# Expert weights in 2 MB tiles, down projections behind the group loop

## The chip, the cores and the metric

The kernel runs on one core of a Trainium2 chip. The metric is device time in microseconds (us) of one execution. A profiled execution also gives a trace of every instruction and transfer; its times are given in us from the start of the span, the span being the time from the first to the last instruction.

## The reference, cut to what matters

Two layers of a transformer-like trunk over 256 tokens of width 1024, all in float32. Each layer has a mixer part (attention with latent keys and values, a stick-breaking attention, a pooling mixer, fed by one input projection and closed by one output projection) and a part of experts: 4 groups of 8, of which each token uses two, so that nearly all experts have some tokens and all their weights are read.

```python
def hybrid_layer(x, ...):
    hn = rms_norm(x, norm1_g)
    proj = jnp.einsum('bsd,df->bsf', hn, w_in)            # 1024 x 1440
    ya = mla_mixer(...); yb = stick_breaking_mixer(...); yc = pool_mixer(...)
    x = x + jnp.einsum('bsm,md->bsd', jnp.concatenate([ya, yb, yc], axis=-1), w_out)
    return x + hier_moe(rms_norm(x, norm2_g), w_group, b_group, w_expert, b_expert, w_gate, w_up, w_down)

def hier_moe(h, ...):                                     # combine: weight of each expert for each token
    ...
    for g in range(N_GROUPS):
        a = jnp.einsum('nd,edf->nef', t, w_gate[g])       # 8 experts, 1024 x 256 each
        b = jnp.einsum('nd,edf->nef', t, w_up[g])
        hid = jax.nn.silu(a) * b * combine[:, g, :, None]
        y = y + jnp.einsum('nef,efd->nd', hid, w_down[g]) # 256 x 1024 each
```

The experts' weights are 96 MB a layer, the other weights of a layer some 12 MB (10^6 bytes); everything is read from HBM once.

## The kernel before

**Weights.** All weights pass through a ring (`Ring`) of 25 slots of 1 MB in SBUF (128 partitions x 2048 float32), which also holds the intermediate tiles (`take`). The order of the transfers, the stream, is written out in `Net.__init__`: w_in (`wa`, `wqk`, `wvu`), the small weights, `uq`, w_out (`wo`), then for each of 8 groups of 4 experts 8 tiles of gate and up weights and 4 tiles of down weights. For the last four groups (`TAIL`) of a layer the down tiles come behind all gate and up tiles, sorted by column quarter, and between the quarters stand the next layer's `wa` and `wqk`. SP issues the transfers. A first, empty pass of the program (`rehearsed`) finds for each transfer the earliest step at which a slot is free for it until its use; in the real pass `tick` issues it there, and SP waits on the chip until the slot's last reader is done.

**Mixers.** The input projection splits weights and activations into two parts each, so that three fast matmuls make one exact one: `split` turns a piece of a weight into its two parts (ScalarE and VectorE, or VectorE and GpSimd), up to three pieces ahead (`AHEAD`). `project_in(l, q, part)` multiplies rows 2q and 2q+1 of `wa` (part 0, 1) and `wqk` (part 2, 3) as soon as column quarter q of x is there. `mixers` then does the eight row blocks of the values and of the pooled part (`values_in`), between the steps Abs, Exp and Ln of the stick-breaking on ScalarE, then head keys, values and queries, attention and the output projection. `route` ends it: routing, and the tokens of the first group gathered into 4 x 32 places (`gather`, by a matmul with a placing matrix d from `place`).

**Experts.** `experts` goes over the 8 groups. `hidden(g)` multiplies 8 tiles; four experts share the array, 32 columns each. `bend` applies SiLU and the expert weight, `collect(g + 1)` gathers the next group's tokens from `hv`, a normalised copy of x, `turn` transposes. For groups 0 to 3 `whole` does the down projection (4 tiles) and adds it to x with a plain matmul (`dT`). Behind group 3 stands `overflow`, a branch for experts with over 32 tokens, not taken here; it claims 5 slots. Groups 4 to 7 keep their hidden values (`th`, `tail`); behind the loop their down projections run by column quarter: `down(g, q)` of one tile, its split into two parts, a scatter of four fast matmuls to the tokens, and once a quarter of x is done, `arrive(l + 1, q)` transposes it for the next layer, whose `project_in` parts run between the items of the next quarter. In the last layer the finished quarter goes to the final norm instead (`leave`), and two idle matmuls stand behind each item (`warm`). The last tile of the stream comes in two halves.

## Time and profile before

| | us |
|---|---|
| median of 3 runs | 603.17 |
| runs | 601.71 to 604.39 |
| the profiled execution | 601.43 |
| its span | 599.8 |
| busy in the span: PE | 526.3 |
| VectorE (DVE) | 261.2 |
| ScalarE (ACT) | 142.7 |
| GpSimd (POOL) | 96.6 |

The transfers are 228.68 MB, of which 93.3% of the 16 transfer engines' time in the span is taken by the queue that SP fills. A matmul's end is modelled in the records, so a busy PE isn't one at its peak, and rows that follow each other may overlap a little. PEclk is the share of the full clock that TensorE was granted: 1.00 is 2.4 GHz, 0.50 is 1.2 GHz.

### The profile page before, as it was taken

What the parts mean: (1) busy time and instruction counts of PE and PEld (TensorE: products, weight loads), DVE (VectorE), ACT (ScalarE), POOL (GpSimd) and SP (SyncE); (2) the same over time, 40 slices, a digit from 0 to 9 for tenths busy, and PEclk for the clock granted to TensorE, in tenths of its full rate; (3) what the DMA queues carried; (4) which work ended last, traced back from release to release, by engine and by line L of the source; (5) the groups of instructions that cost most, each with busy time, mean ns of one, the idle gap of its engine ahead of it and who ended that gap; (6) DMA issues with size and microseconds to landing.
All of it is one profiled execution on the core that took longest, in us unless ns stands there. A gap on an engine that the chain in (4) does not pass through costs nothing. (4 is left out here: it accounts for less than half of the span.)

```text
span 599.8 us, 10395 instructions
## 1 busy us (share of the span) xinstructions
PE 526.3 (88%) x4168; PEld 332.7 (55%) x4168; DVE 261.2 (44%) x644; ACT 142.7 (24%) x339; POOL 96.6 (16%) x138
## 2 busy tenths in 40 slices
PE   8989999898898688679999899998898868886993
PEld 8959877454354144326667787765344424441562
DVE  5879765432332222215357976662332321221242
ACT  4466453200000000013234854322000000001221
POOL 2535223000000000002113442310000000000011
PEclk9999999989999799959999999998999998997998
DMA  8999777999999999999999958689999999999992
GB/s 300 402 419 413 294 281 306 368 389 423 420 420 422 414 422 422 418 423 417 422 419 421 412 200 325 273 325 392 415 423 421 419 419 421 419 422 423 420 398 89
DMA packets 34619, 228.68 MB, mean 381 GB/s; under 512 B 3841, under 2 KB 6145, under 8 KB 7938
## 3 DMA queue, kind: packets, MB, share of 16 engines
q1 hardware_dynamic: 34130, 227.33, 93.3%
q8 instruction: 36, 0.59, 0.4%
q10 hardware_dynamic: 432, 0.59, 0.3%
q14 instruction: 21, 0.17, 0.1%
HBM read 226.85 MB, written 1.05 MB: 380 GB/s over the span
## 5 line engine op out<-in xcount | busy, mean ns | idle before, releaser
L224 PE MATMUL ps<-slot,slot 128*32 128x256 f32 (+6 forms) x3372 | 406.9, 438 | 53.9 <-DVE slot L780 23.2
L224 PEld LDWEIGHTS ps<-slot,slot 128*32 128x32 f32 (+2 forms) x3372 | 242.8, 143 | 187.2 <-issue 94.6
L242 POOL TENSOR_TENSOR slot<-slot,slot 128x512 fp32r<-128x512 f32 (+1 forms) x38 | 50.9, 1339 | 131.0 <-DVE slot L290 54.6
L288 ACT ACTIVATE slot<-ps 128x256 fp32r<-128x256 f32 (+5 forms) x70 | 33.2, 474 | 142.3 <-PE ps L224 128.4
L833 DVE TENSOR_REDUCE ws<-ps 128x1 f32<-128x256 f32 x16 | 6.8, 425 | 131.1 <-PE ps L282 131.1
L224 PE MATMUL ps<-slot 128*128 128x256 f32 (+3 forms) x224 | 58.8, 406 | 0.0
L830 ACT ACTIVATE slot<-ps 128x256 f32<-128x256 f32 x16 | 6.1, 384 | 209.5 <-PE ps L224 209.5
L809 POOL TENSOR_TENSOR slot<-slot,comb 128x128 f32<-128x128 f32 x32 | 12.2, 401 | 266.0 <-PE ps L224 224.8
L242 DVE TENSOR_TENSOR slot<-slot,slot 128x512 fp32r<-128x512 f32 (+1 forms) x54 | 47.4, 880 | 13.9 <-ACT slot L288 13.5
L224 PEld LDWEIGHTS ps<-slot 128*128 128x128 f32 (+1 forms) x224 | 30.2, 193 | 30.8 <-issue 14.4
L793 DVE TENSOR_TENSOR slot<-ps,vec 128x512 f32<-128x512 f32 x32 | 22.1, 692 | 49.5 <-PE ps L224 49.2
L290 DVE COPY slot<-ps 128x512 f32<-128x512 f32 (+3 forms) x30 | 20.5, 690 | 40.9 <-PE ps L224 32.6
L242 DVE TENSOR_TENSOR slot<-ps,slot 128x256 fp32r<-128x256 f32 (+1 forms) x42 | 18.3, 435 | 43.3 <-ACT slot L288 43.2
L288 ACT ACTIVATE slot<-slot 128x512 fp32r<-128x512 f32 (+1 forms) x54 | 33.0, 613 | 15.8 <-PE ps L224 12.8
L282 PE MATMUL ps<-ident,slot 128*128 128x128 f32 x128 | 24.3, 295 | 5.0 <-DVE slot L835 2.9
L282 PEld LDWEIGHTS ps<-ident,slot 128*128 128x128 f32 x128 | 14.8, 144 | 24.2 <-issue 15.4
L863 DVE TENSOR_TENSOR x<-x,ps 128x512 f32<-128x512 f32 x32 | 22.0, 688 | 8.5 <-PE ps L224 8.2
L224 PE MATMUL ps<-ident,ones 128*128 128x128 f32 x108 | 19.1, 312 | 1.6 <-POOL ident L193 1.6
L244 DVE SCALAR_TENSOR_TENSOR slot<-ps,vec,slot 128x256 fp32r<-128x256 f32 x26 | 12.4, 482 | 17.9 <-ACT slot L288 17.8
L288 ACT ACTIVATE slot<-ps,vec 128x256 fp32r<-128x256 f32 x26 | 12.1, 474 | 27.6 <-PE ps L282 13.2
L290 DVE CAST slot<-slot 128x512 fp32r<-128x512 f32 (+1 forms) x38 | 18.5, 487 | 0.0
L224 PEld LDWEIGHTS ps<-ident,ones 128*128 128x128 f32 x108 | 16.0, 216 | 4.0 <-issue 2.4
(126 smaller groups left out, 303.5 us busy)
## 6 DMA issues: line engine op xcount, KB each, us to landing
slot<-in_we SPq DMA_DIRECT2D x191, 1024.0 KB, 19.6
slot<-in_wo SPq DMA_DIRECT2D x8, 1024.0 KB, 19.2
slot<-in_wvu SPq DMA_DIRECT2D x4, 1024.0 KB, 19.8
slot<-in_wqk SPq DMA_DIRECT2D x3, 1024.0 KB, 19.3
slot<-in_wa SPq DMA_DIRECT2D x3, 832.0 KB, 14.2
slot<-in_uq SPq DMA_DIRECT2D x2, 1024.0 KB, 15.2
slot<-in_small SPq DMA_DIRECT2D x2, 784.0 KB, 15.5
x<-in_x SPq DMA_DIRECT2D x4, 256.0 KB, 6.3
```

The source lines that it names most:

```text
L224: self.nc.tensor.matmul(out, lhsT, rhs, start=start, stop=stop, skip_group_check=True)
L242: V.tensor_tensor(lo, in_, hi.bitcast(F32), op=OP.subtract)
L244: V.scalar_tensor_tensor(lo, in_, scale, hi.bitcast(F32), op0=OP.mult, op1=OP.subtract)
L282: self.nc.tensor.transpose(out, in_, self.ident)
L288: nc.scalar.activation(out, in_, AF.Copy, scale=1.0 if scale is None else scale)
L290: nc.vector.tensor_copy(out, in_)
L793: self.nc.vector.tensor_tensor(xs[:, 4 * n:4 * n + 4], v3(self.ps[:, b0 + n], 4, 128), self.vec[:, l, 8 + 4 * n:12 + 4 * n, None].to_broad ...
L809: G.tensor_tensor(d4, d4, comb[:, t, 4 * g:4 * g + 4, None].to_broadcast([128, 4, 32]), op=OP.mult)
L830: A.activation(h, ps[:, 2, 0:256], AF.Silu)
L833: V.tensor_reduce(ws, ps[:, 3, 256:512], axis=AX.X, op=OP.add)
L863: V.tensor_tensor(xs, xs, ps[:, 6 + n], op=OP.add)
```

## The change

- The ring has 11 slots of 2 MB ("pairs") and 3 of 1 MB ("ones"); all weights come in tiles of up to 2 MB (4096 floats a partition), and intermediate tiles that belong together (xH and xL, wH and wL, kT and qT, sH and sL, mH and mL) share a pair. The first tile of the stream comes in three parts, the last in three.
- Groups 0 to 3 have no `whole` any more: the down projections of all 8 groups run behind the loop by column quarters, 32 items a layer.
- Between the items of quarters 1 to 3 of the first layer stands more of the next layer's projection: besides `project_in`'s parts (the two of `wqk` cut in halves) two row blocks of `values_in` a quarter (`behind`). So of layer 1's eight blocks six are done ahead of `mixers`, which then fills the stick-breaking's gaps with head keys, values and queries. There `down` writes one bank (2) instead of two in turn, and the scatter follows in the same item.
- `collect` gathers from x with a scaled placing matrix (`place` makes two: plain and times r2); `hv` is gone, and `overflow` moves from group 3 to behind group 7 and claims three pairs.

```diff
-NSLOT = 25
+NPAIR, NONE = 11, 3
 AHEAD = 3
-TAIL = 4
...
+        r.cut = {"a0.0": ((0, 928),), f"d33.{L - 1}": ((0, 2048), (2048, 3072), (3072, 4096))}
+        rest = [lambda c=c: r.part(*r.stream[0][0:2], *c) for c in ((928, 1856), (1856, 3712))]
+        w(0, "a0", then=[rest[0], load_x(1), rest[1], load_x(2), load_x(3)])
+        w(0, "a1", then=[self.tables])
+        w(0, "v")
         for l in range(L):
-            w(l, "wvu", 0, 1)
-            add(f"sm.{l}", a["small"][l])
-            add(f"uq.{l}", a["uq"][l])
-            w(l, "wo", 3, 2, 0, 1)
-            for g in range(8 - TAIL):
-                we(l, g, *range(12))
-            for g in range(8 - TAIL, 8):
-                we(l, g, *range(8))
+            w(l, "mid", "w0", "w1")
+            for g in range(8):
+                for i in range(4):
+                    add(f"h{g}{i}.{l}", a["wh"][(l * 8 + g) * 4 + i])
             for q in range(4):
...
+                for p in range(4):
+                    add(f"d{q}{p}.{l}", a["wd"][(l * 4 + q) * 4 + p])
+                if l + 1 < L:
+                    w(l + 1, *(("a0", "v"), (), ("a1",), ())[q])
+                elif q == 1:
+                    add("fg", a["fg"])
...
+    def behind(self, q):
+
+        for i in range(2):
+            self.project_in(q, i)
+            yield
+        for i in range(2):
+            w = self.weight()
+            for b in range(2):
+                self.heads_in(2 * q + i, w, (2 * b, 2 * b + 1))
+                yield
+        for i in range(2):
+            self.values_in(2 * q + i)
+            yield
...
+        blocks = deque(range(6 if l else 0, 8))
+        self.values_in(blocks.popleft())
...
+        if l:
+
+            ring.drop("xHL")
+            sH, sL = (v3(t, 4, 384) for t in ring.two("sHL", F32R))
+            values_out()
+            fill = deque([lambda: keys(0), lambda: keys(1), latent_values,
+                          *(lambda j=j: latent_queries(j) for j in range(4))])
+        else:
+            fill = deque([*(lambda k=k: self.values_in(k) for k in blocks)])
...
+    def place(self, g, d, t, pos, r2):
+
+        V = self.nc.vector
+        V.tensor_tensor(d[:, t].rearrange("p (e s) -> p e s", e=4),
+                        self.iota[:, None, :].to_broadcast([128, 4, 32]),
+                        pos[:, t, 4 * g:4 * g + 4, None].to_broadcast([128, 4, 32]), op=OP.is_equal)
+        V.tensor_scalar(d[:, 2 + t], d[:, t], r2[:, t:t + 1], None, op0=OP.mult)
...
-            if i < 0:
-                whole(g, hT, dT)
-            else:
-                tail[g] = hT, dT
-                ring.drop(f"g{g}")
+            turn(g, hT[:, g])
+            ring.drop(f"g{g}")
...
-            if g == 3:
-                self.overflow(l, hv, comb, pos, flag)
-        ring.drop("hn")
+        self.overflow(l, r2, comb, pos, flag)
...
+            beside = self.behind(q - 1) if more and q else None
+            for g in range(8):
+                b = ps[:, 2 if beside else (2, 7)[g % 2], 0:256]
+                down(g, q, b)
+                ys = [parts[:, g % 2 * 2 + p] for p in range(2)]
                 self.parts(*ys, b)
+                if beside:
+                    next(beside)
+                    scatter(g, ys)
+                    continue
                 if prev:
                     scatter(*prev)
-                if l + 1 == L and (q, g) != (3, 7):
+                if not more and (q, g) != (3, 7):
                     self.warm(2, 3)
                 prev = (g, ys)
-                if q and l + 1 < L:
-                    self.project_in(l + 1, q - 1, i)
```

## Rows read from the trace of the kernel before

**Rows 1.** The page: span, transfers, throughput in 40 slices of 15 us (GB/s).

```profile
span 599.8 us, 10395 instructions
...
GB/s 300 402 419 413 294 281 306 368 389 423 420 420 422 414 422 422 418 423 417 422 419 421 412 200 325 273 325 392 415 423 421 419 419 421 419 422 423 420 398 89
DMA packets 34619, 228.68 MB, mean 381 GB/s; under 512 B 3841, under 2 KB 6145, under 8 KB 7938
```

**Rows 2.** Stage table: window and its us; busy us of engines (instructions); PEclk, DMA share, GB/s.

```profile
0.00:58.00 58.00, 53.26 (x331) 47.57 (x331) 43.76 (x85) 32.21 (x67) 25.04 (x38) 1.00 0.98 385
58.00:130.00 72.00, 68.87 (x516) 51.15 (x514) 39.11 (x133) 26.30 (x71) 16.95 (x26) 0.98 0.84 322
130.00:240.00 110.00, 94.12 (x797) 43.63 (x793) 30.80 (x62) 3.71 (x8) 3.80 (x10) 0.97 1.01 420
240.00:340.00 100.00, 86.65 (x679) 57.51 (x678) 49.03 (x108) 33.58 (x77) 20.56 (x20) 0.93 1.01 421
340.00:425.00 85.00, 81.87 (x597) 60.50 (x599) 50.66 (x149) 30.37 (x78) 21.17 (x28) 0.98 0.81 314
425.00:580.00 155.00, 131.51 (x1164) 65.54 (x1156) 40.62 (x90) 12.10 (x28) 6.50 (x14) 0.94 1.01 421
580.00:588.00 8.00, 8.00 (x96) 5.54 (x96) 3.65 (x9) 2.05 (x6) 0.90 (x1) 1.00 0.66 245
```

**Rows 3.** Waits of SP's queue, 345:360: us in total, times, longest.

```profile
SPq L80 <- PE ps L224: 17.6, 1, 17.6
```

**Rows 4.** Timeline of PE (start, us, what): first experts; last output projection, layer 1.

```profile
110.45 7.07 PE L224 MATMUL ps<-slot,slot 128*32 128x512 f32 x64
...
388.97 0.96 PE L224 MATMUL ps<-slot,slot 128*128 128x512 f32 x3
...
400.57 7.07 PE L224 MATMUL ps<-slot,slot 128*32 128x512 f32 x64
```

**Rows 5.** Timeline of PE, layer 0: last hidden tile, then items of quarter 0.

```profile
257.27 1.93 PE L224 MATMUL ps<-slot,slot 128*32 128x512 f32 x8 [1.41 <-DMA slot<-in_we]
...
264.28 1.93 PE L224 MATMUL ps<-slot,slot 128*32 128x256 f32 x16 [0.46 <-DMA slot<-in_we]
...
267.30 1.94 PE L224 MATMUL ps<-slot,slot 128*32 128x256 f32 x16
...
270.32 1.07 PE L224 MATMUL ps<-slot,slot 128*32 128x256 f32 x16
```

**Rows 6.** Timeline of PE: a scatter, quarter ends (transposes), a value block of layer 1.

```profile
290.97 0.74 PE L224 MATMUL ps<-slot 128*128 128x256 f32 x4
...
300.05 0.77 PE L282 MATMUL ps<-ident,x 128*128 128x128 f32 x4 [0.52 <-DVE x L926]
...
313.14 0.77 PE L282 MATMUL ps<-ident,x 128*128 128x128 f32 x4 [0.51 <-DVE x L926]
...
320.08 1.63 PE L224 MATMUL ps<-slot,slot 128*128 128x512 f32 x6
```

**Rows 7.** Busy us (PE, PEld, DVE, ACT, POOL): quarters of layer 0, mixers' first part.

```profile
264.30:313.10 48.80, 46.70 (x424) 31.58 (x424) 22.79 (x51) 13.31 (x35) 8.43 (x7) 0.94 1.01 420
313.10:347.40 34.30, 31.01 (x191) 26.20 (x191) 28.56 (x56) 21.90 (x44) 14.86 (x13) 1.00 0.96 397
```

**Rows 8.** Timeline of PE behind the branch of layer 0.

```profile
204.70 9.12 PE L224 MATMUL ps<-slot,slot 128*32 128x512 f32 x59 [4.26 <-issue]
```

**Rows 9.** Short windows, columns as in rows 2.

```profile
105.00:110.00 5.00, 4.95 (x42) 4.57 (x42) 2.62 (x12) 0.00 (x0) 0.47 (x2) 1.00 1.03 434
262.00:270.00 8.00, 7.54 (x56) 3.44 (x56) 1.55 (x4) 1.15 (x3) 0.00 (x0) 0.50 1.01 420
548.00:552.00 4.00, 2.56 (x12) 0.58 (x4) 1.24 (x3) 1.67 (x2) 0.00 (x0) 0.50 1.01 422
```

**Rows 10.** Timeline of PE: the last two items.

```profile
585.39 1.07 PE L224 MATMUL ps<-slot,slot 128*32 128x256 f32 x16
...
587.50 1.07 PE L224 MATMUL ps<-slot,slot 128*32 128x256 f32 x16
```

More of the change, by code (lines that the diff above doesn't have):

```diff
@@ L50, in __init__, with tile @@
         self.nc, self.pool, self.plan = nc, pool, plan
-        self.idle = deque(range(NSLOT))
-        self.stream, self.issued, self.now, self.cut = [], 0, 0, ()
-        self.live, self.first, self.spans = {}, {}, {}
-    def tile(self, dtype):
-        i = self.idle.popleft()
-        return i, self.pool.tile([128, 2048], dtype, name=f"slot{i}", tag=f"slot{i}")
+        self.idle = {2: deque(range(NPAIR)), 1: deque(range(NONE))}
+        self.stream, self.issued, self.now, self.cut = [], 0, 0, {}
+        self.live, self.first, self.spans, self.kind = {}, {}, {}, {}
+    def tile(self, dtype, n):
+        i = self.idle[n].popleft()
+        name = f"{('one', 'pair')[n - 1]}{i}"
+        return n, i, self.pool.tile([128, 2048 * n], dtype, name=name, tag=name)
     def tick(self):
@@ L62, in tick @@
             name, src, then = self.stream[self.issued]
-            self.live[name] = i, t = self.tile(F32)
-            for i in range(1 if name in self.cut else 2):
-                self.half(name, src, i)
+            self.live[name] = self.tile(F32, 2)
+            for a, b in self.cut.get(name, ((0, src.shape[1]),)):
+                self.part(name, src, a, b)
             self.issued += 1
@@ L68, in tick, with part, take, two @@
                 f()
-    def half(self, name, src, i):
-        p, n = src.shape
-        t = self.live[name][1][:p, :n]
-        if name == self.stream[-1][0]:
-            t, src = (v.rearrange("p (e c n) -> p e c n", e=4, c=2)[:, :, i] for v in (t, src))
-        elif name in self.cut:
-            t, src = (v[:, i * n // 2:i * n // 2 + n // 2] for v in (t, src))
-        elif i:
-            return
-        self.nc.sync.dma_start(t, src)
-    def take(self, name, dtype=F32):
+    def part(self, name, src, a, b):
+        self.nc.sync.dma_start(self.live[name][2][:src.shape[0], a:b], src[:, a:b])
+    def take(self, name, dtype=F32, n=1):
         if self.plan:
-            self.live[name] = self.tile(dtype)
+            self.live[name] = self.tile(dtype, n)
         self.tick()
-        self.first[name] = self.now
-        return self.live[name][1] if self.plan else self.pool
+        self.first[name], self.kind[name] = self.now, n
+        return self.live[name][2] if self.plan else self.pool
+    def two(self, name, dtype=F32):
+        t = self.take(name, dtype, 2)
+        return t[:, 0:2048], t[:, 2048:4096]
     def get(self, name):
@@ L322, in arrive @@
         if q == 0:
-            self.xp = [v3(self.ring.take(n, F32R), 8, 256) for n in ("xH", "xL")]
+            self.xp = [v3(t, 8, 256) for t in self.ring.two("xHL", F32R)]
             self.cw = self.ring.take("cw")
@@ L567, in mixers @@
         breaks(0)
-        mixed = [v3(ring.take(n, F32R), 8, 256) for n in ("mH", "mL")]
+        mixed = [v3(t, 8, 256) for t in ring.two("mHL", F32R)]
         mH, mL = mixed
-        small = ring.get(f"sm.{l}")
+        small = ring.get(f"mid.{l}")
         for wi in range(4):
@@ L734, in route @@
         land(1, 1)
-        ring.drop("mH", "mL", "wH", "wL")
+        ring.drop("mHL", "wHL")
         by_tokens(0)
```

378 lines of the change are left out of this document (177 added, 201 removed).

## The prediction, as it was put on record

> **What bounds the kernel now.** I read the page's slices of DMA throughput first, then a table of busy time and throughput by stage, then what SyncE (SP), which issues the weight transfers, waits for, then TensorE (PE) in order of time at the places where it changes from waiting to not waiting.
>
> The slices of 15 us show 420 GB/s again and again, and two valleys, one in each layer's mixers [rows 1]. The stage table puts sizes to them: 420 and 421 GB/s in both group loops and in the tail between, 322 in 58:130 and 314 in 340:425 [rows 2]. All 228.68 MB [rows 1] at 421 would take 543 us; the other 57 us of the span are time in which the transfer engines stood. Of that (421-385)/421 x 58 = 5 us is the start, (421-322)/421 x 72 = 17 us the first valley, (421-314)/421 x 85 = 22 us the second, and about 13 us the end, where the last column quarter is worked off and stored. So the kernel's time is the weight stream plus the valleys. In a valley the ring of slots is full and SP waits for PE to free one, 17.6 us at a stretch [rows 3]: PE works through the mixers (PE busy 81.87 of 85 us, [rows 2]) and eats few weights. A valley ends when PE begins the experts of the layer, at 110.45 and 400.57 (call the second T1) [rows 4], because from there it frees 8 MB in 7.07 us, far faster than 421 GB/s fills them.
>
> From this the rule for the end: **the end is T1 plus what the stream still owes then.** And T1 is PE's: PE last waits for weights at 257.27 and, half a microsecond, at 264.28 [rows 5]; behind that it works to 400.57 with no transfer ending its waits. The 136 us between are what the change rebuilds.
>
> **The change part by part.**
>
> *Slots in pairs.* 25 slots of 1 MB become 11 of 2 MB and 3 of 1 MB. Before the layer's first expert 24 slots could hold weights (one holds g0); afterwards 11 pairs, 22 MB. The last two pairs come free with mHL and wHL, when the output projection's last matmuls end at 388.97+0.96 = 389.9, that is 10.6 us ahead of T1 [rows 4]; 4 MB (4.19e6 bytes) need 10.0 us, so the ring is full again about at T1, and the next pair is free a quarter of 7.07 us later. I allow 1 us more from there to flowing data (no row prices it: 0 to 2). So at T1+3 the stream has delivered 11 pairs of experts, 23.1 MB, and goes on.
> Layer 0, same offsets: at 113.5 it has 13.4 MB of everything ahead of the experts (counted from the arrays) and 23.1, so 36.5 MB, and at 130 43.4 MB. Before, 58 us at 385 and 72 at 322 make 45.5 MB at 130 [rows 2]. The loss is 2.1 MB, **5.0 us** (3 to 7, as the frees inside the mixers come pairwise).
>
> *2 MB transfers.* Bytes are the same. Each row of a tile is 16 KB and there are half as many transfers. A steady stage runs at 420 to 421 [rows 2]; single 5 us windows reach 434 [rows 9]. So the gain lies between 0 and 3%; I take 1%, nearer to the long steady rows than to one short window. The 1 MB transfers overlap: at 421 GB/s one lands every 2.5 us.
> The Trainium skill ("DMA: Bandwidth & Descriptors", Measured) gives 341 GB/s for a 1 MB transfer and 425 for 16 MB, and a fixed 2 us for each. By that, about 110 transfers fewer would save over 200 us, if none overlapped. The stage rows disagree: 1 MB transfers already stream at 421, so the fixed part is hidden, and the sum goes by the rows.
>
> *Down projections behind the loop.* A group's `whole` leaves the loop. That frees PE time where the stream is late anyhow: a group's hidden weights are 8 MB, 20 us of stream, for 7.07 us of hidden matmuls [rows 4] and a gather, and PE had caught up with the stream before 257.27 even with four `whole` in the loop [rows 5]. Nothing is gained there. The extra scaling in `place` (two small VectorE operations a group) and the removed `hn` lie under the same wait. The branch of `overflow` moves from group 3 to behind group 7; it stood 4.26 us in PE's way [rows 8]. It takes three pairs, which leaves 7, 35 us of stream, in flight: SP passes it long before these are landed, so nothing; if SP stood there longer than that, each us would count.
> At its new place PE then has eight items (group, quarter) of quarter 0, at 3.02 us with the half clock (264.28 to 267.30, clock 0.50 in 262:270) or about 1.75 with the full one (1.07 and 0.74) [rows 5, 6, 9], against 2.5 us of stream for each. The start of quarter 1 therefore hangs on a transfer, d10, the first of that quarter. **When does it land?** Up to its end the stream has 13.4 MB, 64 MB of hidden weights (67.1e6 bytes), quarter 0 (8.4), a0 (1.9), v and d10 (2.1 each), 95.0 MB; up to the tile whose matmuls start at 257.27 it had 13.4 and 80 tiles of 1 MB, 97.3. So 2.3 MB less, -5.5 us; the front's loss, +5.0; 1% on the 140 us between, -1.4: **255.4**.
>
> *Quarters 1 to 3 of layer 0.* Before, a quarter is 13.09 us (transposes at 300.05 to those at 313.14), with four items and four parts of the next projection [rows 6]. Afterwards it has eight items and two value blocks more: 4 x (1.07 + 0.74) for down and scatter [rows 5, 6], 2 x 1.63 for the blocks [rows 6], together 10.5; rows overlap at their modelled ends, I take 10.0. **23.1 us a quarter** (22.5 to 24.5: the single bank 2 puts ScalarE's and VectorE's split of a result between down and scatter, and a piece of projection covers it). VectorE was busy 22.79 of 48.8 us there and ScalarE 13.31 [rows 7], so they have room. A quarter's stream is 8 MB, 20 us: PE is late, not the weights. 255.7 + 69.3 = **325.0** for the transposes that stood at 313.14.
>
> *Mixers of layer 1.* Six of eight value blocks are gone: 6 x 1.63 = 9.8 us of PE. But 313.1:347.4 isn't PE's alone: VectorE is busy 28.56 of 34.3 us, ScalarE 21.90 [rows 7]. With the blocks go their splits; the stick-breaking's Abs, Exp and Ln, the head copies and the other splits stay in line on these two. So the gain is between 3 us (both stay the bound) and 12 (all of the blocks' time and the gaps beside them); I take **5**, nearer to the lower, by VectorE's row. T1 = 325.0 + (400.57 - 313.14) - 5 = **407.4**, 6.8 later.
>
> *The end.* Before, 155 x 421 + 8 x 245 = 67.2 MB were owed at 425, 24.4 us behind T1 [rows 2]. Afterwards at T1+24.4: 100.7 - 23.1 - 21.4 x 0.421 = 68.6. So +3.3 us, less 1% on 160, -1.6: +1.7. In the last stage PE has 32 items of 2.11 us (585.39 to 587.50) against 2.5 of stream, so it follows the stream, and the last transfer, cut alike, is followed by the same half a down, split, scatter and store; before, PE began its last item at 587.50 without a wait [rows 10], so there is little to win here.
>
> **Sum** against the profiled execution: span 599.8 + 6.8 + 1.7 = 608.3; outside the span it had 601.43 - 599.8 = 1.6, and it lay 1.7 below the median 603.17. So **611** for the median.
>
> **The rivals.**
> *1. The next projection really is free and wide rows stream faster.* Against me speaks that the six blocks do leave the valley, and that 434 GB/s has been seen [rows 9]. With 22.5 a quarter, 12 us off the mixers, 3% on the stream: d10 at 252.6, T1 = 252.9 + 67.5 + 87.4 - 12 = 395.8, the end -4.8 +3.3 -4.8 = 593.5, median **597**. It decides from T1 below about 397. For it, the valley's PE rows; against it, VectorE's.
> *2. The two sides cancel.* Half of each: mixers 8 us shorter, 2% on the stream: T1 = 254.3 + 68.4 + 87.4 - 8 = 402.1, end +1.5 +3.3 -3.2, median **605**, within the bound.
> *3. PE falls to the half clock where it waits tile by tile.* A row shows clock 0.50 at 548:552, where PE waits for weights, and half-speed items at 264 to 267 [rows 5, 9]; the work itself brings the clock back (1.07 instead of 1.93 at 270.32). The change makes two more such stages. If all of quarter 1 ran like 264.28 (3.03 for 1.75), 8 x 1.3 = 10 us and some 4 for the projection would be added to T1: median **625**. I take it for unlikely, since quarter 1 is dense. The Trainium skill ("TensorE: Matmul & The Clock Gate", HAM oscillation) tells of a kernel that turns cold at each tile because its matmuls are shorter than the wait for the next; by that rule quarter 0 and the last stage run cold; the row at 270.32 agrees only so far as the stage is sparse.
> *4. The wide transfers change nothing in the rate.* Then +3.0 on the sum, **614**; it is inside my case.
>
> **How the numbers follow.** My case (606 to 618): 0.64, of which 0.03 reach under 606. Rival 1 0.13, rival 2 0.18 (0.01 of it under 600), rival 3 0.05. The forecast is my case's 611. Its terms reach from 601 (with rival 2's and a part of rival 1's) to 618; that leaves out most of rivals 1 and 3, about 2 in 10. A measurement of this kernel tells about 0.5% from no change, so 600.2 to 606.2 is the same: faster 0.14, same 0.20, slower 0.66.
>
> **What would show it.** Throughput about 425 in the loops (rate); quarters of 23 us and a first wait-free stretch from about 256 to 407 on PE; layer 1's first expert at 407; a second valley longer than 22 us although fewer blocks stand in it. I am wrong if PE still waits for weights in quarters 1 to 3 (then the stage is free), if T1 is at 400 or earlier, or if SP stands at the branch and the stream has a hole at 225 to 260.

## The result and the profile after

| | before | after |
|---|---|---|
| median, us | 602.44 (4 runs, 600.05 to 604.39) | 630.87 (4 runs, 630.48 to 631.68) |
| span of the profiled execution, us | 599.8 | 628.9 |

The ratio is 1.048, interval 1.043 to 1.052: slower, as forecast, but by 28 us instead of 8, and outside the forecast range of 601 to 618. Where one execution lay over 1.5% above the fastest of its kernel (once each in runs 4, 9 and 10 below; in run 10 it took 1037.91 us), medians and ratios here are without it. The page of the profile after, the lines that answer to [rows 1]:

```profile
span 628.9 us, 10437 instructions
...
GB/s 319 417 422 244 267 269 287 350 399 426 428 426 430 423 425 425 428 429 422 431 427 425 68 209 271 214 348 430 428 428 426 426 428 426 424 427 426 425 153 68
DMA packets 18444, 228.69 MB, mean 364 GB/s; under 512 B 2129, under 2 KB 3409, under 8 KB 4690
```

The plateaus are higher than before, both valleys are deeper, and the last slice but one shows 153 where before it showed 398. The stage table (columns as in [rows 2]; only the last stretch is cut otherwise):

```profile
0.00:58.00 58.00, 51.60 (x310) 44.80 (x311) 40.54 (x82) 31.24 (x66) 22.67 (x36) 0.97 0.94 380
58.00:130.00 72.00, 69.42 (x484) 52.39 (x487) 41.98 (x136) 24.66 (x70) 19.14 (x28) 0.98 0.72 282
130.00:240.00 110.00, 88.50 (x704) 47.65 (x700) 27.19 (x68) 4.73 (x10) 4.79 (x12) 0.89 1.00 422
240.00:340.00 100.00, 88.89 (x813) 61.23 (x810) 38.51 (x94) 25.92 (x71) 16.68 (x14) 0.96 1.01 427
340.00:425.00 85.00, 78.15 (x524) 59.13 (x522) 54.76 (x152) 38.11 (x92) 20.62 (x30) 0.96 0.61 237
425.00:580.00 155.00, 123.03 (x1030) 68.72 (x1034) 36.91 (x93) 10.54 (x25) 6.52 (x15) 0.89 1.01 427
580.00:626.00 46.00, 39.95 (x452) 26.43 (x444) 15.15 (x38) 10.26 (x27) 3.54 (x4) 0.97 0.54 226
```

By 130 us the stream has delivered 380 x 58 + 282 x 72 = 42.3 MB, 3.2 MB less than before (45.5); by 425 us 151.6 MB against 160.5. The second valley carries 237 GB/s instead of 314, though fewer value blocks stand in it.

TensorE's timeline (start, us, what, wait and its releaser) at the points of [rows 4 to 6] and [rows 10]: first expert of layer 0, behind the branch, first item of quarter 1, ends of quarters 1 to 3, first expert of layer 1, the end of quarter 0 in the last layer, and the last item.

```profile
113.36 7.07 PE L211 MATMUL ps<-pair,one 128*32 128x512 f32 x64
...
235.13 3.64 PE L211 MATMUL ps<-pair,one 128*32 128x256 f32 x32 [6.77 <-PEq L966]
...
257.94 1.93 PE L211 MATMUL ps<-pair,one 128*32 128x256 f32 x16 [5.32 <-DMA pair<-in_wd]
...
281.90 0.66 PE L273 MATMUL ps<-ident,x 128*128 128x128 f32 x4 [0.85 <-DVE x L941]
...
306.71 0.66 PE L273 MATMUL ps<-ident,x 128*128 128x128 f32 x4 [0.84 <-DVE x L941]
...
330.27 0.66 PE L273 MATMUL ps<-ident,x 128*128 128x128 f32 x4 [0.85 <-DVE x L941]
...
416.95 7.07 PE L211 MATMUL ps<-pair,one 128*32 128x512 f32 x64
...
554.99 0.72 PE L211 MATMUL ps<-pair 128*128 128x256 f32 x4
563.61 3.78 PE L211 MATMUL ps<-pair,ones 1*128 1x512 f32 x4 [7.90 <-DMA pair<-in_fg]
...
617.41 1.07 PE L211 MATMUL ps<-pair,one 128*32 128x256 f32 x16
```

The forecast against these, in its own steps:

| step | forecast | measured | difference |
|---|---|---|---|
| quarter 1's first item starts | 255.7 | 257.94 | +2.2 |
| quarters 1 to 3 | 69.3 | 72.3 | +3.0 |
| last transposes to first expert (T1) | 82.4 | 86.7 | +4.3 |
| T1 | 407.4 | 416.95 | +9.5 |
| T1 to the end of the span | 200.9 | 212.0 | +11.1 |
| span | 608.3 | 628.9 | +20.6 |

The first and the fourth of these rows hold some chance: the kernel of run 1 below differs only behind T1 and has quarter 1's first item at 256.78 and T1 at 414.00.

Two rows point to causes that no step of the forecast has. In the last stage PE stands 7.90 us for `fg`, the final norm's weights, and from there to the end no transfer ends a wait of PE. And the chain of waits, which before ran on PE and on the weights, goes in one piece through that transfer (the second number is the length of each piece in us):

```profile
537.29 26.28 DMA pair<-in_fg
563.56 0.04 issue
563.61 56.35 PE ps L211 x576
```

### The profile page after: what moved, and what is told of

Its sections match the earlier page's. It is cut to its first block, busy times and chain, and to the rows that moved or that the text cites. A ratio compares the mean times of both kernels' runs of the same rounds, so it can differ in the third digit from the quotient of the medians.

```text
span 628.9 us, 10437 instructions
## 1 busy us (share of the span) xinstructions
PE 539.5 (86%) x4296; PEld 360.4 (57%) x4296; DVE 255.0 (41%) x660; ACT 145.5 (23%) x359; POOL 94.0 (15%) x138
## 5 line engine op out<-in xcount | busy, mean ns | idle before, releaser
L211 PE MATMUL ps<-pair,one 128*32 128x256 f32 (+2 forms) x2060 | 190.9, 502 | 19.9 <-PEq L966 13.4
L211 PE MATMUL ps<-pair,pair 128*128 128x512 f32 (+2 forms) x576 | 126.3, 365 | 4.0 <-POOL pair L229 2.3
L211 PEld LDWEIGHTS ps<-pair,one 128*32 128x32 f32 (+1 forms) x2060 | 62.4, 113 | 113.6 <-issue 87.8
L211 PEld LDWEIGHTS ps<-pair,pair 128*128 128x128 f32 x576 | 93.9, 192 | 28.7 <-issue 10.1
L211 PE MATMUL ps<-one,x 128*128 128x128 f32 x512 | 78.5, 317 | 29.1 <-DVE one L819 28.7
L211 PEld LDWEIGHTS ps<-one,x 128*128 128x128 f32 x512 | 72.1, 225 | 35.9 <-DVE one L819 35.7
L229 POOL TENSOR_TENSOR pair<-pair,pair 128x512 fp32r<-128x512 f32 (+1 forms) x38 | 49.4, 1300 | 172.2 <-DVE pair L281 111.6
L211 PE MATMUL ps<-pair 128*128 128x256 f32 (+1 forms) x320 | 61.3, 314 | 1.5 <-DVE low L560 0.6
L211 PEld LDWEIGHTS ps<-pair 128*128 128x128 f32 x320 | 46.0, 193 | 20.7 <-issue 15.8
L229 DVE TENSOR_TENSOR pair<-pair,pair 128x512 fp32r<-128x512 f32 (+1 forms) x54 | 46.6, 866 | 23.9 <-ACT pair L279 23.2
## 6 DMA issues: line engine op xcount, KB each, us to landing
pair<-in_mid SPq DMA_DIRECT2D x2, 1808.0 KB, 20.6
```

The costliest lines, as they stand in the source:

```text
L211: self.nc.tensor.matmul(out, lhsT, rhs, start=start, stop=stop, skip_group_check=True)
L229: V.tensor_tensor(lo, in_, hi.bitcast(F32), op=OP.subtract)
```

## The experiments

Unless it says otherwise a kernel is the changed one with the edit shown. The kernel before, run again beside each group of experiments, has medians of 602.2 to 602.9. Further down "the two mends" are those of runs 1 and 3.

**1. `fg` ahead of quarter 1.** The old order puts `fg` in front of the four down tiles of quarter 1; the change appends it behind them. `leave(0)` wants it at the end of quarter 0.

```diff
             for q in range(4):
+                if l + 1 == L and q == 1:
+                    add("fg", a["fg"])
                 for p in range(4):
                     add(f"d{q}{p}.{l}", a["wd"][(l * 4 + q) * 4 + p])
                 if l + 1 < L:
                     w(l + 1, *(("a0", "v"), (), ("a1",), ())[q])
-                elif q == 1:
-                    add("fg", a["fg"])
```

> The changed kernel with one line moved: the final norm's gain (fg) stands in the weight stream ahead of the 8 MB of quarter 1's down weights of the last layer, as in the kernel before, instead of behind them. Theory A (the stream order of fg costs at the end): PE waited 7.90 us for fg at 555.7 to 563.6, then ran its items of 2.11 us without a wait and was done 16 us behind the last transfer. Without the wait PE follows the stream; the last transfer lands at about 603 as in the changed kernel, the end comes 12 to 13 us behind it, span 616 (-12 to -13 us). Rival B (PE's items are the bound of the last stage with or without fg, for instance since each wait for a tile drops the clock): span above 622.

618.94 (617.16 to 621.08), ratio 1.029 (1.025 to 1.033), span 615.6. The same matmul of the last stage now waits for nothing:

```profile
553.53 1.98 PE L211 MATMUL ps<-pair,ones 1*128 1x512 f32 x4
```

12 us by the medians came from one small transfer in the wrong place of an in-order queue. From T1 (414.00) to the end it is 201.6 us instead of 212.0, against the forecast's 200.9; that stretch alone, the only one in which `fg` can act, is 10.4 us shorter. So that step's size was right, without the order that it overlooked.

**2. The mirror in the kernel before.** There `fg` goes behind quarter 1's tiles.

```diff
                 if l + 1 == L:
-                    if q == 1:
-                        add("fg", a["fg"])
+                    pass
...
                 for g in range(8 - TAIL, 8):
                     we(l, g, 8 + q)
+                if l + 1 == L and q == 1:
+                    add("fg", a["fg"])
```

> The kernel before with fg behind quarter 1's down tiles of the last layer instead of ahead of them: the mirror of the first run, to see the price of that order by itself. PE should stand at the end of quarter 0 until fg has landed, with 12 items of 2.11 us behind it (25 us) against 8 tiles of 2.5 us still owed (20 us): 5 to 9 us slower than before, median 607 to 611. If the order were without effect here: 602.

606.99 (602.08 to 610.16), ratio 1.007 (1.003 to 1.011). PE does wait there:

```profile
565.33 3.78 PE L225 MATMUL ps<-slot,ones 1*128 1x512 f32 x4 [3.30 <-DMA slot<-in_fg]
```

The price is 4.3 us, a little under the 5 to 9 expected. The order is the same, the price isn't: the wait is 3.30 us instead of 7.90, and 12 items are left behind it instead of 24. A reading that fits both, though no run separates the two, is that the wait costs what PE can't win back: the more PE work is left behind it, the less of it lies under the rest of the stream.

**3. Stick-breaking copies later**, on top of run 1. ScalarE's copy of the stick-breaking matrix (L506) waits for GpSimd's triangle mask (L462). In the change it stands inside the fill loop, ahead of splits that PE's next matmuls need.

```diff
...
                 earlier(sp[:, i])
-            if l:
-                stick_parts(h)
         while fill:
             fill.popleft()()
+        if l:
+            stick_parts(2)
```

(`stick_parts(0)` moves behind the second of the head queries.)

> On top of the moved fg: in layer 1's mixers the two ScalarE copies of the stick-breaking parts (with GpSimd's subtractions) are issued later, the first behind the second block of head queries, the second behind the last, as they stood in the kernel before. Theory A (queue order: ScalarE stands 1.67 and 3.40 us for GpSimd's select at those copies, and weight splits, query products and scores queue behind it): the mixers get 3 to 4 us shorter and the time falls by as much. Rival B (the mixers gain nothing from the blocks taken out because VectorE's and ScalarE's own work is the bound there): within 1 us of the kernel with the moved fg.

616.39 (612.94 to 618.21), ratio 1.024 (1.020 to 1.029), span 611.3. ScalarE's timeline of the changed kernel, the two copies and what follows each:

```profile
354.53 0.84 ACT L506 ACTIVATE pair<-one 128x768 fp32r<-128x768 f32 x1 [1.67 <-POOL one L462]
355.28 0.61 ACT L279 ACTIVATE pair<-pair 128x512 fp32r<-128x512 f32 x1
...
362.12 0.84 ACT L506 ACTIVATE pair<-one 128x768 fp32r<-128x768 f32 x1 [3.40 <-POOL one L462]
362.87 0.61 ACT L279 ACTIVATE pair<-pair 128x512 fp32r<-128x512 f32 x1
```

and with the copies later:

```profile
351.80 0.85 ACT L506 ACTIVATE pair<-one 128x768 fp32r<-128x768 f32 x1 [0.35 <-POOL one L462]
352.56 0.83 ACT L525 ACTIVATE one<-one 128x768 f32<-128x768 f32 x1
...
357.50 0.85 ACT L506 ACTIVATE pair<-one 128x768 fp32r<-128x768 f32 x1 [2.72 <-POOL one L462]
358.25 0.39 ACT L567 ACTIVATE one<-one,low 128x128 f32<-128x128 f32 x1
```

Directly behind the first copy now stands no split, and behind the second one none that PE is waiting for. From the last transposes (327.63) to T1 (409.73) it is 82.1 us; the changed kernel has 86.7, run 1 has 85.3, the forecast said 82.4. The ends of this sum, and the wait for quarter 1's first tile (d10):

```profile
255.59 1.93 PE L211 MATMUL ps<-pair,one 128*32 128x256 f32 x16 [6.59 <-DMA pair<-in_wd]
...
327.63 0.66 PE L273 MATMUL ps<-ident,x 128*128 128x128 f32 x4 [0.85 <-DVE x L942]
```

The forecast's 5 us for six blocks fewer were right in this trace; the order of ScalarE's queue had taken 3 to 4 of them back. The medians of runs 1 and 3 are 2.6 us apart and their intervals overlap, so the gain rests on the mixers' stretch of the trace more than on the whole time.

**4. The value blocks back in layer 1's mixers**, on top of run 1: `behind` without `values_in`, the mixers of layer 1 in the order of layer 0.

```diff
-            if l and q < 3:
-                value(2 * q)
-                value(2 * q + 1)
-        for k in range(6 if l else 0, 8):
+        for k in range(8):
             value(k)
...
-        for i in range(2):
-            self.values_in(2 * q + i)
-            yield
```

> On top of the moved fg: the six value blocks of layer 1 go back from the quarters into the mixers, whose order is then that of layer 0 in both layers; the rest of the change stays. Theory A (the blocks cost their full PE time in the quarters and gave next to nothing back in the mixers): quarters of 21 us instead of 24.3, mixers (from the last transposes to the first expert) 2 us longer, the first expert of layer 1 at 409 instead of 417, time 7 to 8 us below the kernel with the moved fg. Rival B (the blocks are worth their PE time in the mixers): mixers 9 us longer, time the same.

631.07 (625.86 to 631.80), ratio 1.044 (1.036 to 1.052), which fits neither theory. Quarter 2 of layer 0 has a hole of 9 us on PE:

```profile
299.43 1.49 PE L211 MATMUL ps<-pair 128*128 128x256 f32 x4 [8.99 <-ACT pair L276]
```

and ScalarE's row says why:

```profile
298.55 0.55 ACT L276 ACTIVATE pair<-pair 128x416 fp32r<-128x416 f32 x1 [11.37 <-DMA pair<-in_a]
299.01 0.37 ACT L276 ACTIVATE pair<-ps 128x256 fp32r<-128x256 f32 x1
```

The split of a weight piece that is three pieces ahead waits for `a1`, and the split of the down result that PE wants now stands behind it. With the value pieces gone from the feed, "three pieces ahead" reached a tile that the stream has behind quarter 2. So the run tells nothing of the value blocks; it shows the same mechanism as run 3, with a transfer in GpSimd's place.

**5. The same without that hole**, and with the copies late (they are, in layer 0's order).

```diff
-                    w(l + 1, *(("a0", "v"), (), ("a1",), ())[q])
+                    w(l + 1, *(("a0",), ("a1",), ("v",), ())[q])
```

> The changed kernel with fg first, the six value blocks back in the mixers of layer 1, and the next projection's tiles by need: a0 behind quarter 0, a1 behind quarter 1, v behind quarter 2. The stall of 8.99 us of the run with the values back should be gone if it was a1's transfer (ScalarE's split for the pieces ahead waits for it). Theory A (the value blocks between the items cost PE as much as they give back, and v in front of quarter 1 costs its transfer): quarter 1 begins at 253 instead of 257.94, quarters of 21 to 22.4 us, first expert of layer 1 at 403 to 408, median 606 to 613. Theory B (the blocks between the items are a gain, as forecast): at least 3 us slower than the run with the stick-breaking copies later (616.39).

619.97 (618.82 to 622.99), ratio 1.029 (1.025 to 1.034). Last transposes at 328.06, T1 at 416.29: 88.2 us of mixers. Against run 3 the last transposes are equal (327.63), the mixers 6.1 longer, the median 3.6. The quarters didn't get shorter with less work in them, except the first: in the other two PE waits for down tiles.

```profile
279.38 1.92 PE L211 MATMUL ps<-pair,one 128*32 128x256 f32 x16 [2.60 <-DMA pair<-in_wd]
...
303.89 1.94 PE L211 MATMUL ps<-pair,one 128*32 128x256 f32 x16 [0.96 <-DMA pair<-in_wd]
```

This points to theory B: the mixers lose about what the forecast said, and the time between the items is no worse for the blocks. The whole time alone doesn't show it, since the intervals of runs 3 and 5 overlap, and the tiles' order differs too.

**6. Half-size transfers** on top of run 1: every tile over 2048 columns goes in two transfers, rows of 8 KB as before, slots unchanged.

```diff
-            for a, b in self.cut.get(name, ((0, src.shape[1]),)):
+            n = src.shape[1]
+            for a, b in self.cut.get(name, ((0, n // 2), (n // 2, n)) if n > 2048 else ((0, n),)):
```

> On top of the moved fg: each tile of up to 2 MB comes by two transfers of half its columns (rows of 8 KB), slots and order unchanged. Theory A (the wide rows are what raised the steady rate from 420.5 to 426 GB/s): rate back at 420 to 421, 1.2% of the some 350 us of stream on the path, 4 to 5 us slower than the kernel with the moved fg. Rival B (the rate comes from something else, such as the order in HBM): rate 426, same time.

619.46 (616.74 to 620.09), ratio 1.028 (1.023 to 1.032); the interval overlaps that of run 1 (1.025 to 1.033). The loops of the last layer, run 1 and then this one:

```profile
425.00:580.00 155.00, 130.80 (x1177) 74.09 (x1177) 39.83 (x99) 13.77 (x34) 6.70 (x14) 0.93 1.01 427
```
```profile
425.00:580.00 155.00, 132.15 (x1178) 75.71 (x1178) 39.72 (x99) 13.36 (x33) 7.17 (x16) 0.94 1.01 420
```

The size of the transfers makes the rate: 427 GB/s with 2 MB in rows of 16 KB, 420 with 1 MB in rows of 8 KB (row length and size go together here). In the span it is 1.8 us, in the median 0.5, which can't be told from nothing.

**7. The down projections behind the loop alone, in the kernel before** (`TAIL` = 8, one more tile for the split results, 1 MB slots, value blocks in the mixers).

```diff
-TAIL = 4
+TAIL = 8
...
-                th, tw = ring.take("th"), ring.take("tail", F32R)
+                th, tw, tp = ring.take("th"), ring.take("tail", F32R), ring.take("tailp", F32R)
...
-        parts = v3(tw, 4, 256, 1024)
+        parts = v3(tp, 4, 256)
...
-                if q and l + 1 < L:
-                    self.project_in(l + 1, q - 1, i)
+                if q and l + 1 < L and i % 2:
+                    self.project_in(l + 1, q - 1, i // 2)
```

> The kernel before with one part of the change alone: the down projections of all 8 groups behind the loop (TAIL = 8, one tile more for the split results), in 1 MB tiles, with all eight value blocks of layer 1 still in its mixers. Theory A (the move itself is no loss: the weight stream carries the loop, and the first quarter now begins after fewer bytes): first tile of quarter 1 of layer 0 has 90.8 MB ahead of it instead of 97.3 MB up to the tile at 257.27, so about 242 us; quarters of 20.3 us (8 items of 1.81 and the four parts), held by the stream at 22; last transposes at about 305 instead of 313.14, first expert of layer 1 at 391 to 394, median 594 to 598. Theory B (the price of the change is this move): eight items a quarter instead of four make the stretch in which PE is alone longer, first expert of layer 1 at 405 or later, median 607 or more.

610.69 (610.59 to 611.23), ratio 1.014 (1.011 to 1.016). T1 is 405.06, between the two theories. The mixers are as before (87.4 us); the last transposes come at 317.65 instead of 313.14. T1 is 4.5 us later than before, and from T1 to the end it is 204.0 us instead of 199.2. What is lost up to T1 went at the first experts of layer 0, where the stream slows to 86 GB/s. The stretch 100:115, before first and then here:

```profile
100.00:115.00 15.00, 14.51 (x128) 9.83 (x130) 9.17 (x42) 3.52 (x9) 2.64 (x9) 1.00 0.87 332
```
```profile
100.00:115.00 15.00, 14.51 (x127) 10.40 (x127) 9.35 (x43) 4.51 (x11) 1.91 (x8) 1.00 0.29 86
```

That is 3.7 MB less. The tiles for the hidden values and the split results are now claimed from group 0 on instead of group 4, three slots of the ring. So the move alone isn't free; that its cost is these slots is argued from the code and from this stretch, and fits the price in run 8.

**8. What buffer is worth: the kernel before with 23 slots.**

```diff
-NSLOT = 25
+NSLOT = 23
```

> The kernel before with 23 slots instead of 25 and nothing else: the price of 2 MB of buffer. If the stream stands in each layer's mixers with every slot full, each slot fewer leaves 1 MB (2.5 us of stream) to be fetched later, in both layers: 5 us by the first expert of layer 1 and 5 at the end, median 609 to 613. If the buffer is not what binds: 602 to 604.

611.25 (609.57 to 613.70), ratio 1.015 (1.011 to 1.019): 8.7 us for 2 MB. T1 is 408.32 instead of 400.57.

**9. The whole change in 1 MB tiles**: both mends, but 25 slots of 1 MB, weights in tiles of 1 MB, `a` and `v` in parts, each where it is needed.

```diff
-NPAIR, NONE = 11, 3
+NSLOT = 25
...
     def two(self, name, dtype=F32):
-        t = self.take(name, dtype, 2)
-        return t[:, 0:2048], t[:, 2048:4096]
+        return self.take(name + "/0", dtype), self.take(name + "/1", dtype)
...
+                for g in range(8):
+                    half(f"d{q}{g}.{l}", a["wd"][(l * 4 + q) * 4 + g // 2], g % 2)
+                    if l + 1 < L:
+                        if (q, g) in ((1, 0), (3, 0)):
+                            half(f"v{q // 2}.{l + 1}", a["v"][l + 1], q // 2)
+                        if (q, g) in ((0, 7), (1, 4), (2, 4), (3, 4)):
+                            pa(l + 1, q)
```

> The whole change without the pairs: all down projections behind the loop, all of the next projection between, fg first, the stick-breaking copies later, but 25 slots of 1 MB with tiles of 1 MB, as before; v in halves where they are needed. Theory A (the 2 MB slots and tiles are what still costs the 14 us of the run with fg first and the later copies: fewer tiles held at the first expert, a0 and v in front of quarter 1): the first tile of quarter 1 lands at about 245 (90.9 MB ahead of it at 420 GB/s, one slot fewer at the first expert), three quarters of 24 to 24.5, mixers of 82, first expert of layer 1 at 399 to 402, median 599 to 604. Theory B (the order is what costs, whatever the tiles): first expert of layer 1 at 408 or later, median 611 to 617.

601.28 (median of 11), ratio 0.999 (0.997 to 1.002): the same as before, theory A. Its first valley, the second one and the loop behind it, and then those of run 3, which has the pairs:

```profile
58.00:130.00 72.00, 69.43 (x488) 51.70 (x490) 42.04 (x137) 23.64 (x69) 18.79 (x27) 0.98 0.81 306
...
340.00:425.00 85.00, 78.93 (x561) 56.48 (x560) 49.23 (x151) 28.88 (x76) 22.96 (x34) 0.98 0.85 329
425.00:580.00 155.00, 135.66 (x1268) 78.56 (x1267) 40.79 (x101) 16.54 (x42) 7.01 (x14) 0.94 1.01 420
```
```profile
58.00:130.00 72.00, 69.42 (x501) 50.32 (x503) 41.74 (x136) 23.65 (x68) 18.79 (x27) 1.00 0.74 291
...
340.00:425.00 85.00, 78.92 (x560) 60.51 (x560) 53.90 (x155) 36.84 (x89) 22.72 (x32) 0.98 0.67 261
425.00:580.00 155.00, 132.64 (x1208) 75.62 (x1196) 39.13 (x98) 14.54 (x36) 6.70 (x14) 0.93 1.01 426
```

T1 is at 400.96 with 1 MB tiles and at 409.73 with pairs:

```profile
400.96 7.07 PE L224 MATMUL ps<-slot,slot 128*32 128x512 f32 x64
```

So with the two mends the pairs, with the order that whole tiles of 2 MB force on the stream, cost 616.4 - 601.3 = 15 us, and everything else that the change does costs nothing in sum.

**10. The pairs' order in 1 MB tiles**: both halves of `a0` and of `v` behind quarter 0, those of `a1` behind quarter 2.

```diff
-                        if (q, g) in ((1, 0), (3, 0)):
-                            half(f"v{q // 2}.{l + 1}", a["v"][l + 1], q // 2)
-                        if (q, g) in ((0, 7), (1, 4), (2, 4), (3, 4)):
-                            pa(l + 1, q)
+                if l + 1 < L and q in (0, 2):
+                    pa(l + 1, q)
+                    pa(l + 1, q + 1)
+                    for i in range(2 if q == 0 else 0):
+                        half(f"v{i}.{l + 1}", a["v"][l + 1], i)
```

> The change in 1 MB tiles (601.3) with the next projection's tiles in the order that the pairs have: both tiles of a0 and both of v behind quarter 0, both of a1 behind quarter 2. Theory A (this order is a good part of the 15 us): 3 MB more in front of quarter 1's first tile, 7 us, of which PE had about 5 to spare; first expert of layer 1 at 403 to 407, median 603 to 608. Theory B (it is the capacity alone): unchanged, 600 to 602.5.

606.40 (median of 9, 604.91 to 608.21), ratio 1.006 (1.004 to 1.008), T1 407.55: theory A. Against run 9 the order costs 5.1 us by the medians and 3.9 by the ratios, so 4 to 5 of the 15.

**11. The 1 MB version with 23 slots** (run 8's edit).

> The change in 1 MB tiles with 23 slots instead of 25. If a slot is worth here what it was in the kernel before (8.7 us for two): median 608 to 611, with first expert of layer 1 4 us later. If the new order needs the buffer less: 602 to 605.

612.32 (609.77 to 612.57), ratio 1.015 (1.012 to 1.019), T1 405.12: 2 MB of buffer are worth 11.0 us by the medians and 9.5 by the ratios, at least what they were in the kernel before. How much buffer the pairs lose can be read from the traces, as MB transferred from the start of the span (GB/s times us):

| | 20 us behind layer 0's first expert | 24.4 us behind T1 |
|---|---|---|
| run 9, 25 slots | 342 x 132.4: 45.3 | 378 x 425.4: 160.8 |
| run 10, the pairs' order | 339 x 133.4: 45.2 | 371 x 432.0: 160.3 |
| run 11, 23 slots | 324 x 133.4: 43.2 | 369 x 429.5: 158.5 |
| run 3, pairs | 331 x 132.0: 43.7 | 366 x 434.1: 158.9 |

Behind both valleys the pairs stand nearly as low as the ring that is 2 MB smaller, and the order alone costs next to nothing there. The code gives a reason: from the first group on the loop holds a pair for `tp` (10 pairs, 20 MB, are left for weights, against 21 slots of 1 MB), and a pair comes free only when both its halves are read. By the table the pairs lose about 0.8 of what two slots fewer lose, an estimated 7 to 9 us; with 4 to 5 for the order, and less up to 1.8 for the rate, that makes 9 to 14 for the 15 measured. So the buffer is the larger part; that the parts add up like this was not run, and what is left of the 15 is open.

**12. `v` later in the pairs** (with both mends): `v` behind d10 instead of in front of it, and the first tile of the stream cut by the order of use.

```diff
-        r.cut = {"a0.0": ((0, 928),),
+        r.cut = {"a0.0": ((0, 416), (928, 1344)),
...
+                    if l + 1 < L and (q, p) == (1, 0):
+                        w(l + 1, "v")
...
-                    w(l + 1, *(("a0", "v"), (), ("a1",), ())[q])
+                    w(l + 1, *(("a0",), (), ("a1",), ())[q])
```

> The changed kernel with fg first and the stick-breaking copies later, and two more orders mended: v comes behind the first down tile of quarter 1 instead of in front of it, and the first tile of the stream is cut by the order in which its columns are used. Theory A: quarter 1 begins 4 to 5 us earlier than 255.6 (2.1 MB at 427 GB/s), the first expert of layer 0 at 112 instead of 113.4, first expert of layer 1 at 403 to 406 instead of 409.73, median 609 to 613. If the transfer in front of quarter 1 isn't what it waits for, or the quarter's later tiles are: first expert of layer 1 at 408 or later, median 614 to 617.

617.92 (616.37 to 619.52): no gain, my theory A fell. PE waits 1.09 us for d10 instead of 6.59, and then 4.11 for the next tile:

```profile
253.85 1.93 PE L213 MATMUL ps<-pair,one 128*32 128x256 f32 x16 [1.09 <-DMA pair<-in_wd]
265.17 1.94 PE L213 MATMUL ps<-pair,one 128*32 128x256 f32 x16 [4.11 <-DMA pair<-in_wd]
```

Moving 2 MB one tile back moves the wait one tile back. The order of run 10 differs in more: there the halves of `a` and `v` are spread over all the quarters. The cut of the first tile did nothing that can be read either: the first expert is at 114.13. In the runs that have the order of the kernel before up to there, 110.45 and 112.17 (run 8) were seen, so a microsecond or two at that place isn't told from chance.

**13. PE's steps in the loop, in the 1 MB version**: the next group placed before the hidden matmuls, the branch behind group 6.

```diff
         for g in range(8):
+            if 0 < g < 7:
+                seats(g + 1)
             hidden(g)
...
-        self.overflow(l, r2, comb, pos, flag)
+            if g == 6:
+                self.overflow(l, r2, comb, pos, flag)
```

(`seats` is `collect`'s placing, taken out of it.)

> The change in 1 MB tiles (601.3) with two steps taken out of PE's way in the loop: VectorE places group g+1 before the hidden matmuls of group g instead of behind them (each gather waited 1.96 us for it), and the branch stands behind group 6, when the last gather has read x, instead of behind group 7 (6.63 us of PE). Theory A (in 1 MB tiles PE, not the stream, sets the pace up to quarter 1, against the forecast): the end of quarter 0 in layer 0 at 238 to 242 instead of 246.46, first expert of layer 1 at 393 to 397 instead of 400.96, median 594 to 598, faster than the kernel before. Theory B (the stream carries that stretch, as forecast): unchanged, 600 to 602.5.

603.29 (median of 12), ratio 0.999 (0.997 to 1.002), as in run 9: theory B. PE gets ahead by group 6 and then waits for every tile; quarter 1's items are held too (250 to 264; first expert of layer 1 at 402.53):

```profile
188.22 1.07 PE L224 MATMUL ps<-slot,slot 128*32 128x512 f32 x8 [0.36 <-DMA slot<-in_wh]
...
251.54 11.78 PE L224 MATMUL ps<-slot,slot 128*32 128x256 f32 x104 [2.09 <-DMA slot<-in_wd]
```

So the forecast's step that PE has time to spare in layer 0 up to quarter 1 holds, and the branch of 6.8 us behind group 7, longer than the 4.26 of [rows 8], is covered: the stream runs on at 422 GB/s in 130:240 of the changed kernel, and PE waits for d10 after it.

**14 and 15. The pairs alone** (down projections of groups 0 to 3 in the loop, value blocks in the mixers), tried twice. The main lines of both:

```diff
+        def whole(g):
+            ys = st[g][1].rearrange("p k s -> p (k s)")
+            for q in range(4):
+                down(g, q, ps[:, 4 + q // 2, q % 2 * 256:q % 2 * 256 + 256])
...
-            for g in range(8):
+            for g in range(4, 8):
```

("The preceding kernel" is that of run 5.)

> The preceding kernel with the down projections of groups 0 to 3 in the loop again (in its tile order: the tile of two groups comes behind the first one's hidden weights; results summed in a tile of their own and added to x quarter by quarter). So 2 MB tiles and slots in pairs alone, against the kernel before. Theory A (the pairs are what costs: coarser slots, a0 in one tile in front of quarter 1): first quarter with four items, quarters of 13 to 14 us, first expert of layer 1 at 404 to 410, median 606 to 613. Theory B (the pairs are free and the faster stream pays): median 597 to 602.

> The pairs alone, without the flaw of the earlier run of that kind (there four tiles of 2 MB were held for two groups): here groups 0 to 3 have their down weights in two tiles of 2 MB each, used at once and dropped, in the loop as before; value blocks in the mixers; groups 4 to 7 behind the loop. Theory A (the pairs cost): first expert of layer 0 at 112 to 113, less held there (two pairs are kept for the loop's own results), first expert of layer 1 at 405 to 411, median 606 to 614. Theory B (the pairs are free and the rate of 427 pays): median 597 to 602.

656.59 and 643.45, worse than the whole change, so neither prices the pairs alone. In the first, four down tiles of 2 MB are held for two groups. The second mends that, but its loop still keeps two pairs for its own results, and its stream has delivered 4.5 MB less by 130 us than that of the kernel before; its branch lies uncovered in front of quarter 0:

```profile
267.35 1.92 PE L214 MATMUL ps<-pair,one 128*32 128x512 f32 x16 [1.99 <-DMA pair<-in_wh]
...
277.95 3.64 PE L214 MATMUL ps<-pair,pair 128*32 128x256 f32 x32 [6.43 <-PEq L982]
```

A quarter takes 15.4 to 16.6 us there instead of 13.1, which I didn't trace further. The price of the pairs is therefore read from the other side, from run 9 against run 3.

## Why the prediction was right in sign and wrong in size

- **What bounds the kernel**: "the end is T1 plus what the stream still owes then" did not hold in the changed kernel, where 212.0 us lie behind T1, since PE had work left when the stream was done. With `fg` moved (run 1) it holds: 201.6 us, forecast 200.9.
- **The end: PE "follows the stream", and "there is little to win here".** This step failed, by 10 us in the trace and 12 in the medians. It asked only what the last items cost and not what stands between them: `fg`, moved behind four tiles of 2 MB in the diff, which holds PE for 7.90 us with 24 items still to do. It put the order of the small transfers at nothing without a reason.
- **Mixers of layer 1, 5 us shorter.** This step failed too. The size was right (run 3: 82.1, forecast 82.4). What failed is that ScalarE and VectorE were counted by busy time alone, not in their order. The change put a copy that waits for GpSimd ahead of splits, and 3 to 4 of the 5 us were gone (its waits are 1.67 and 3.40 us).
- **Quarters of 23.1 us.** Mis-sized by 1 us each: 24.1 on average. The third, the least disturbed, takes 23.56, which is the old 13.09 and the full 10.5 of the forecast's own rows; the overlap by which it took 10.0 isn't there. The first item of quarter 1 runs at the half clock after PE's wait for d10 (1.93 for 1.07; granted clock 0.60 in 257.9:262), and quarter 2 waits once for its splits (0.61 and 0.19).
- **Slots in pairs, 5.0 us at the front.** The right mechanism, too small: the loss at 130 us is 3.2 MB instead of 2.1. Counted from the first expert the forecast was near: 20 us behind it 43.3 MB have come (325 GB/s over 133.4 us), where its sum gives 43.6. The rest is that the first expert came 2.9 us later than before (113.36; 112.77 and 112.04 in runs 1 and 3), which the forecast put at nothing; why is open, and some of it may be chance (run 12). No run prices the 1 us "to flowing data" or the pair `tp`, which the count of 11 left out, by itself. d10 came 2.2 us later than forecast in this trace, 1.1 later in run 1 and on time in run 3. At the second valley the +3.3 was nearly right (run 1: 201.6 to the end at a better rate).
- **Rate.** 427 against 420.5, +1.5% for the forecast 1%. The sum credits its 1% with 3.0 us; run 6 finds at most 1.8 for the 1.5%.
- **Down projections behind the loop: nothing gained.** Not shown by itself. Run 9, which has them there with the rest of the change, is as fast as the kernel before; alone (run 7) the move cost 8 us.
- **The sum.** Its own terms add up to 611.7, not 611; that changes nothing.
- **Rivals.** Rival 3 (the half clock) is seen only behind waits: 3.78 instead of 1.98 us for the matmul behind `fg` (granted clock 0.50 in 563.5:567.5). It is a part of what these waits cost, not a case of its own. Neither quarter 0 (1.07 for an item's down matmuls from 241.91 on) nor the last stage (granted clock 1.00 in 570:600 of run 1) ran cold as a whole. Rivals 1 and 2 went with T1.

After the two mends the kernel stands at 616.4, 5 us above the forecast 611 and inside its range. By the medians the 20 us that the forecast missed are thus 12 for `fg`, some 3 for the copies and 5 for the rest. Of these 5 the trace of run 3 shows 2.7 in the quarters (72.0 for 69.3) and 0.7 behind T1; the traced execution was the fastest of its four, 3.5 us below their median. None of the versions beats the kernel before.

## What to carry to other kernels

When a diff rewrites the order of a queue, write both orders out side by side and ask of every entry, the small ones too, who waits for it and what now stands ahead of it: a transfer of 4 KB cost 12 of the 28 us here, and an engine's in-order queue does the same with one operation that waits for a slow neighbour. A kernel that streams weights through a full buffer is priced in megabytes held at the moment when the consumer comes back; here 1 MB was worth 4 to 5.5 us, more than the whole measured gain in rate from transfers twice as large, so coarser slots have to pay for themselves first. Where work is taken off an engine, the gain is visible only if what replaces it at the head of the other queues doesn't wait.

## What the runs showed of the hardware

- Transfers of 2 MB in rows of 16 KB stream at 427 GB/s where those of 1 MB in rows of 8 KB stream at 420, and splitting the same tiles into two transfers of 8 KB rows takes it back (run 6). The Trainium skill ("DMA: Bandwidth & Descriptors", Measured) has 341 GB/s for a transfer of 1 MB; here a stream of such transfers runs at 420.
- At the branch that isn't taken PE stands 4.3 us in the middle of the loop before ([rows 8]), and 6.4 to 6.8 us behind group 7 (6.43 in run 15, 6.77 in the changed kernel).
- Behind waits of 3.30, 5.32 and 7.90 us PE's next matmuls took about twice the time (3.78 for 1.98, 1.93 for 1.07), at the 1.2 GHz level: the granted clock is 0.50 in 563.5:567.5, behind the wait of 7.90. Without the wait (run 1) the same matmul took 1.98, at a granted clock of 1.00 in 553.5:555.6.
